# Large products beside a recurrence, issued two k tiles at a time

## The chip, the core and the metric

The kernel runs on one core of a Trainium2 chip. TensorE (PE, its weight loads shown as PEld), VectorE (DVE), ScalarE (ACT), GpSimd (POOL) and the queues of transfers work side by side; each takes its own instructions in order and waits for the others by semaphores. The metric is the device time of one execution in microseconds.

## What is computed

Two layers of a diffusion backbone over 256 context tokens and 512 latent tokens with 1024 channels, in float32. In each layer one input projection feeds three branches: a bidirectional RWKV-7 recurrence of 16 heads of 64, a convolution of width 31, and attention of 8 heads; gates merge them, and an MLP follows. The last layer needs the latent tokens alone. Cut to what matters here:

```python
def _rwkv_scan(state0, r, decay, k, v, kk, a, reverse):
    def step(S, inp):
        r_t, w_t, k_t, v_t, kk_t, a_t = inp
        s_kk = jnp.einsum('bhij,bhj->bhi', S, kk_t)
        S = (S * w_t[:, :, None, :]
             - s_kk[..., None] * (kk_t * a_t)[:, :, None, :]
             + v_t[..., None] * k_t[:, :, None, :])
        return S, jnp.einsum('bhij,bhj->bhi', S, r_t)
    ...
def token_mixer(hc, hl, ..., w_in, ...):
    zc = hc @ w_in          # 1024 x 10112, cut into the branches' parts
    zl = hl @ w_in
```

## The kernel before

All tokens lie along the free axis, channels on partitions. A large product takes 128 columns of a weight: for each of 8 k tiles it multiplies the high and low halves of a split operand and a split weight (`hh,wh`, `hl,wh`, `hh,wl`) in fast float32 (fp32r), so 3 matmuls a k tile and piece of tokens. With all 768 tokens there are two pieces of 384 columns, so 6 matmuls a k tile; with the latent tokens alone one piece of 512, so 3. Weights come in halves of 4 k tiles: ACT rounds one (L328, `wh`), DVE forms the rest (L332, `wl`).

The recurrence is done in chunks of 64 tokens, 12 of them, for a pair of heads at a time; there are 8 pairs a layer, and both directions run together. For each pair: inputs and decays; front groups (L828, six, 64x128 weights) whose masked outputs go to DVE (L832); the inverse of 32x32 blocks on DVE (`rw_solve`, from the transposition L886 over 30 times L891 and L892 to the transpositions L895 and L896); two merges on PE (L928, then L939, 32x32); batches (L955, L966, 64x64); the chain of 12 states (L987, 128x64, and L991, L1006, 64x64, with ACT at L993); and the readout. The next pair's front groups wait for a part of the chain. These small matmuls are plain float32, and most use a part of the array.

While this goes on, the input projection's products are issued as filler. `job` puts a product's 8 k tiles into a list, `fill(n)` issues the next n of them. `weave` runs generators in turns: each tells how many microseconds it has used, `pe` turns them into k tiles by a ratio, and `taps` issues in the same way the convolution's 31 taps of each channel block (L472 and L469, on DVE, pinned behind whatever was written ahead of them). A product's outputs go to its `done` function; for the convolution that is `done_a` (L462 writes `u`, which the taps read), for the recurrence's inputs `shift_done` (shift additions, L656). The attention also calls `fill(1)` between its steps.

The program is not issued in the order in which it is written. A scheduler goes through it and takes for each engine the first instruction that is ready by its own reckoning; among ready ones, what stands earlier in the program comes first, and what is written under high priority comes before the rest.

Of the kernel before, what the change touches and what calls it, by code (L numbers as in the profile page):

```python
# [19 lines left out]
KT = 8  # L20
# [56 lines left out]
class Kern:  # L77
# [319 lines left out]
    def fill(s, n=1):  # L397
        nc = s.nc
        for _ in range(min(n, len(s.jobs))):
            k, mh, ml, T, done, pre = s.jobs.pop(0)  # L400
            if k % 4 == 0:
                while s.halves and len(s.ready) < s.nw:
                    s.ready.append(s.weight_half(*s.halves.pop(0)))
                s.cur = s.ready.pop(0)
            if k == 0:
                s.jps = s.mm()
                s.jctx = (pre(),) if pre else ()
            wh, wl = s.cur
            for w, m, f in ((wh, mh, 0), (wh, ml, 1), (wl, mh, 2)):
                a = m(k)  # L410
                for b, t0, t1 in s.pieces(T):
                    s.last_mm = nc.tensor.matmul(s.jps[:, b, :t1 - t0], lhsT=w[:, k % 4, :], rhs=a[:, t0:t1], start=k == 0 and f == 0, stop=k == KT - 1 and f == 2)  # L412
            if k == KT - 1:
                done(s.jps, *s.jctx)

    def pe(s, us):

        s.debt += us * s.ratio
        n = int(s.debt)
        s.fill(n)  # L420
        s.debt -= n

# [1071 lines left out]
```

## Time and profile before

| | us |
|---|---|
| median of three runs | 4302.82 |
| the runs | 4300.85 to 4306.18 |
| the profiled execution | 4305.05 |
| its span | 4303.3 |
| PE busy | 4083.1 |
| DVE busy | 2712.4 |
| ACT busy | 1829.2 |

The first layer's recurrence lies at about 165 to 1330 us, its attention up to 1535, the merge of the branches and the MLP up to 2486, the second layer's recurrence at 2530 to 3540, its attention up to 3703, and merge and MLP behind it. A row in order of time gives start, duration, engine, line, operation, output and inputs by the program's names, the weights' shape, the shape that streams, and how many such instructions are put together; in brackets the idle time ahead and what ended it. Matmuls overlap, so the time between two starts tells what one costs, not the durations.

### The profile page before, as it was taken

To read this page: it belongs to the slowest core of one execution; us is meant where nothing else is said; L and a number is where in the kernel's file an instruction comes from. 1 tells how busy PE (TensorE), PEld (TensorE's weight loads), DVE (VectorE), ACT (ScalarE), POOL (GpSimd) and SP (SyncE) were. 2 spreads that over 40 slices of the span, in tenths; PEclk is the share of its full clock that TensorE was granted. 3 is DMA by queue.
4 is the path that set the end of the run, shared out by engine and by line. 5 is a ranking of instruction groups with operands and counts; after the bars stand their busy time and mean duration, and the time that the engine had idled before them with its cause. 6 is when DMAs were issued, how large, how long until landed. Compare 5 with 4: busy or idle time off the path is not lost.

```text
span 4303.3 us, 76623 instructions
## 1 busy us (share of the span) xinstructions
PE 4083.1 (95%) x31232; PEld 3360.6 (78%) x31232; DVE 2712.4 (63%) x5126; ACT 1829.2 (43%) x3426; POOL 254.8 (6%) x221
## 2 busy tenths in 40 slices
PE   6999999999998989899999899999999989898998
PEld 4988888888886679689999677877777765575886
DVE  3788888898855554332233478788889855554344
ACT  3444444444434442332222355455555534433332
POOL 0000000000001022100000200000000000121001
PEclk8999999999999999999999899999999979998998
DMA  4212221112134234343332131112122232242332
GB/s 167 80 49 63 59 62 57 49 55 71 58 102 165 70 116 154 126 147 118 101 98 62 64 90 54 55 59 59 59 65 61 84 125 76 68 138 61 96 96 79
DMA packets 443591, 367.70 MB, mean 85 GB/s; under 512 B 19662, under 2 KB 391528, under 8 KB 437096
## 3 DMA queue, kind: packets, MB, share of 16 engines
q1 hardware_dynamic: 422504, 283.10, 21.9%
q10 hardware_dynamic: 20736, 79.70, 5.1%
q8 instruction: 247, 4.05, 0.4%
q14 instruction: 104, 0.85, 0.1%
HBM read 301.38 MB, written 53.48 MB: 82 GB/s over the span
## 4 chain that ended last, share of the span: by engine, by line
PE 78%; DVE 11%; ACT 4%; issue 3%; DMA 2%; POOL 2%; SPq 0%; ACTq 0%; DVEq 0%; POOLq 0%
PE mm L412 29%; PE mm L389 21%; PE g L828 3%; PE g L634 2%; PE g L955 2%; PE g L966 2%; PE sp L987 2%; PE sp L991 2%; PE S L613 1%; PE g L875 1%; PE g L1071 1%; PE yp L1006 1%; DVE wl L332 1%; DVE A L892 1%; DVE Z L891 1%
## 5 line engine op out<-in xcount | busy, mean ns | idle before, releaser
L328 ACT ACTIVATE wh<-raw 128x512 fp32r<-128x512 f32 x700 | 441.4, 631 | 1218.4 <-PE mm L389 562.9
L332 DVE TENSOR_TENSOR wl<-raw,wh 128x512 fp32r<-128x512 f32 x700 | 500.6, 717 | 692.8 <-ACT wh L328 678.6
L412 PE MATMUL mm<-hh,wh 128*128 128x384 f32 (+1 forms) x2072 | 658.9, 378 | 10.0 <-ACT hh L347 4.0
L412 PE MATMUL mm<-hl,wh 128*128 128x384 f32 (+1 forms) x2072 | 626.0, 362 | 7.2 <-POOL hl L330 7.2
L412 PE MATMUL mm<-hh,wl 128*128 128x384 f32 (+1 forms) x2072 | 619.1, 361 | 2.5 <-DVE wl L332 2.4
L472 DVE SCALAR_TENSOR_TENSOR cv<-u,dw,cv 128x783 f32<-128x783 f32 (+1 forms) x480 | 426.7, 889 | 1.5
L412 PEld LDWEIGHTS mm<-hh,wh 128*128 128x128 f32 x2072 | 367.8, 191 | 61.8 <-issue 9.8
L412 PEld LDWEIGHTS mm<-hl,wh 128*128 128x128 f32 x2072 | 383.9, 191 | 34.4 <-POOL hl L330 10.0
L412 PEld LDWEIGHTS mm<-hh,wl 128*128 128x128 f32 x2072 | 384.0, 192 | 29.8 <-DVE wl L332 4.5
L412 PE MATMUL mm<-oh,wh 128*128 128x384 f32 (+1 forms) x768 | 252.3, 383 | 10.4 <-DVE acc L1320 6.0
L412 PE MATMUL mm<-ol,wh 128*128 128x384 f32 (+1 forms) x768 | 240.0, 365 | 10.6 <-POOL ol L330 10.6
L389 PE MATMUL mm<-hh,wh 128*128 128x384 f32 (+1 forms) x768 | 239.1, 366 | 6.3 <-ACT hh L347 3.6
L389 PE MATMUL mm<-hl,wh 128*128 128x384 f32 (+1 forms) x768 | 238.2, 365 | 5.5 <-POOL hl L330 5.0
L412 PE MATMUL mm<-oh,wl 128*128 128x384 f32 (+1 forms) x768 | 239.4, 365 | 0.0
L389 PE MATMUL mm<-hh,wl 128*128 128x384 f32 (+1 forms) x768 | 235.8, 362 | 0.0
L389 PE MATMUL mm<-fh,wh 128*128 128x384 f32 (+1 forms) x768 | 230.0, 353 | 0.0
L389 PE MATMUL mm<-fh,wl 128*128 128x384 f32 (+1 forms) x768 | 229.9, 353 | 0.0
L389 PE MATMUL mm<-fl,wh 128*128 128x384 f32 (+1 forms) x768 | 229.5, 352 | 0.0
L412 PEld LDWEIGHTS mm<-oh,wh 128*128 128x128 f32 x768 | 139.9, 190 | 51.5 <-ACT wh L328 13.6
L993 ACT ACTIVATE S<-sp,lam 128x64 f32<-128x64 f32 x352 | 94.4, 310 | 192.1 <-PE sp L991 172.4
L389 PEld LDWEIGHTS mm<-hh,wh 128*128 128x128 f32 x768 | 142.2, 192 | 37.7 <-ACT wh L328 15.9
L892 DVE TENSOR_TENSOR A<-A,Z 128x30 f32<-128x30 f32 (+14 forms) x480 | 159.0, 331 | 12.2
(300 smaller groups left out, 7078.5 us busy)
## 6 DMA issues: line engine op xcount, KB each, us to landing
raw<-in_w_in_dram SPq DMA_DIRECT2D x316, 256.0 KB
raw<-in_w_ff_dram SPq DMA_DIRECT2D x256, 256.0 KB
wmod<-in_w_mod_dram ACTq DMA_DIRECT2D x48, 1024.0 KB
raw<-in_w_branch_dram SPq DMA_DIRECT2D x96, 256.0 KB
z<-f ACTq DMA_DIRECT2D x40, 384.0 KB
gt<-z SPq DMA_DIRECT2D x24, 384.0 KB
raw<-in_w_out_dram SPq DMA_DIRECT2D x32, 256.0 KB
z<-f ACTq DMA_DIRECT2D x32, 256.0 KB
```

The costliest lines, as they stand in the source:

```text
L328: s.last_hi = nc.scalar.activation(out=hi, in_=src, func=AF.Copy)
L332: nc.vector.tensor_tensor(out=lo, in0=src, in1=hi.bitcast(F32), op=ALU.subtract)
L389: nc.tensor.matmul(ps[:, b, :t1 - t0], lhsT=w[:, k % 4, :], rhs=a[:, t0:t1], start=k == 0 and f == 0, stop=k == KT - 1 and f == 2)
L412: s.last_mm = nc.tensor.matmul(s.jps[:, b, :t1 - t0], lhsT=w[:, k % 4, :], rhs=a[:, t0:t1], start=k == 0 and f == 0, stop=k == KT - 1 and ...
L472: s.tap_pin(nc.vector.scalar_tensor_tensor(out=hold['c'], in0=u[:, k:k + L], scalar=w(k), in1=hold['c'], op0=ALU.mult, op1=ALU.add))
L634: nc.tensor.matmul(op[:, :nq], lhsT=V[:, kk, kv * 128:kv * 128 + 128], rhs=PT[:, kk, :nq], start=kk == 0, stop=kk == nk // 128 - 1)
L828: nc.tensor.matmul(gp[h][:, q, 0:n, :], lhsT=BK[ROWS[h], 4 * g + q].rearrange("p a b -> p (a b)"), rhs=E[ROWS[h], 0:n, 4 * g + q, :], star ...
L892: nc.vector.tensor_tensor(out=X[:, k + 1:, 0:k], in0=X[:, k + 1:, 0:k], in1=tm, op=ALU.add)
L955: nc.tensor.matmul(wu[ROWS[h], q - q0], lhsT=TT[ROWS[h], q, :], rhs=KM[ROWS[h], q].rearrange("p a b -> p (a b)"), start=True, stop=True)
L966: nc.tensor.matmul(ap[ROWS[h], q - q0, 0:n, :], lhsT=W[ROWS[h], q, :], rhs=GB[ROWS[h], h, q, 0:n, :], start=True, stop=True)
L987: nc.tensor.matmul(sp[ROWS[h], d], lhsT=GB[d][:, h, q[d], 0, :], rhs=UV[d][:, h * 12 + q[d], :], start=d == 0, stop=d == 1 and k == 0)
L993: nc.scalar.activation(out=Sn[:, d], in_=sp[:, d], func=AF.Copy, scale=Q['lam', d][:, q[d]:q[d] + 1])
```

## The change

`fill` gathers the matmuls of a k tile in a list. At an even k the first of them is issued as before; the others, and all of the odd k tile that follows, are issued under high priority. `pe` issues only even numbers of k tiles and keeps the odd one as debt. Neither the matmuls nor their operands change.

```diff
--- before.py
+++ after.py
@@ -406,17 +406,23 @@
                 s.jps = s.mm()
                 s.jctx = (pre(),) if pre else ()
             wh, wl = s.cur
-            for w, m, f in ((wh, mh, 0), (wh, ml, 1), (wl, mh, 2)):
-                a = m(k)
-                for b, t0, t1 in s.pieces(T):
-                    s.last_mm = nc.tensor.matmul(s.jps[:, b, :t1 - t0], lhsT=w[:, k % 4, :], rhs=a[:, t0:t1], start=k == 0 and f == 0, stop=k == KT - 1 and f == 2)
+            run = [(w, m, f, p) for w, m, f in ((wh, mh, 0), (wh, ml, 1), (wl, mh, 2)) for p in s.pieces(T)]
+
+            def issue(ps):
+                for w, m, f, (b, t0, t1) in ps:
+                    s.last_mm = nc.tensor.matmul(s.jps[:, b, :t1 - t0], lhsT=w[:, k % 4, :], rhs=m(k)[:, t0:t1], start=k == 0 and f == 0, stop=k == KT - 1 and f == 2)
+            if k % 2 == 0:
+                issue(run[:1])
+                run = run[1:]
+            with s.tc.high_priority():
+                issue(run)
             if k == KT - 1:
                 done(s.jps, *s.jctx)
 
     def pe(s, us):
 
         s.debt += us * s.ratio
-        n = int(s.debt)
+        n = int(s.debt) // 2 * 2
         s.fill(n)
         s.debt -= n
```

In the changed program L412 becomes L413, and each later line's number is higher by 6.

Two places in the order. PE in the first layer's recurrence, in the chain of states (`sp`, `yp`) beside batches (`GB`, `BK`); `mm` are the large products. Before:

```order
L412 MATMUL mm<-hh,wh 128x384
L966 MATMUL g<-GB_683,BK_680 64x128 x8
L412 MATMUL mm<-hh,wh 128x384
L412 MATMUL mm<-hl,wh 128x384 x2
L412 MATMUL mm<-hh,wl 128x384 x2
L1040 MATMUL g<-cst,y 128x128 x3
L987 MATMUL sp<-UV_679,GB_678 64x64 x2
L987 MATMUL sp<-UV_684,GB_683 64x64 x2
L991 MATMUL sp<-S,KR_676 64x64 x2
L991 MATMUL sp<-S,KR_681 64x64 x2
L1006 MATMUL yp<-S,KR_676 64x64 x2
L1006 MATMUL yp<-S,KR_681 64x64 x2
```

In the changed program, in the same part:

```order
L413 MATMUL mm<-hh,wl 128x384 x2
L713 MATMUL g<-cst,A 128x128 x3
L972 MATMUL g<-GB_678,BK_675 64x128 x8
L993 MATMUL sp<-UV_679,GB_678 64x64 x2
L993 MATMUL sp<-UV_684,GB_683 64x64 x2
L997 MATMUL sp<-S,KR_676 64x64
L972 MATMUL g<-GB_683,BK_680 64x128 x8
L997 MATMUL sp<-S,KR_676 64x64
L997 MATMUL sp<-S,KR_681 64x64 x2
L1012 MATMUL yp<-S,KR_676 64x64 x2
L1012 MATMUL yp<-S,KR_681 64x64 x2
L413 MATMUL mm<-hh,wh 128x384 x2
```

Runs of one to six large matmuls between small groups have become runs of twelve; the small groups between them stand together, and a batch now stands inside a step of the chain. Over the whole program PE goes from a small group to large products 953 times before and 547 times now.

DVE in the inverse of the sixth pair of the first layer; `A` and `Z` are its two buffers, `cv` is the convolution's sum. Before:

```order
L891 TENSOR_TENSOR Z<-A 128x108
L892 TENSOR_TENSOR A<-A,Z 128x27x4
L332 TENSOR_TENSOR wl<-raw,wh 128x512
L891 TENSOR_TENSOR Z<-A 128x130
L892 TENSOR_TENSOR A<-A,Z 128x26x5
L891 TENSOR_TENSOR Z<-A 128x150
L892 TENSOR_TENSOR A<-A,Z 128x25x6
```

In the changed program:

```order
L898 TENSOR_TENSOR A<-A,Z 128x19x12
L475 TENSOR_SCALAR cv<-u,dw,V 128x783
L897 TENSOR_TENSOR Z<-A 128x234
L478 SCALAR_TENSOR_TENSOR cv<-u,dw,cv 128x783
L898 TENSOR_TENSOR A<-A,Z 128x18x13
L478 SCALAR_TENSOR_TENSOR cv<-u,dw,cv 128x783
L897 TENSOR_TENSOR Z<-A 128x238
L478 SCALAR_TENSOR_TENSOR cv<-u,dw,cv 128x783
```

Before, splits of weights stand between the steps of this inverse and no tap; now taps alternate with the steps, 21 of them in this pair, and shift additions stand there too.

## Rows read from the trace of the kernel before

**Rows 1.** The page's part 1: engine, busy us (share of the span) xinstructions.

```profile
PE 4083.1 (95%) x31232; PEld 3360.6 (78%) x31232; DVE 2712.4 (63%) x5126; ACT 1829.2 (43%) x3426; POOL 254.8 (6%) x221
```

**Rows 2.** Windows of both recurrences: length, then busy us of PE, PEld, DVE, ACT, POOL.

```profile
223.00:1195.00 972.00, 966.86 (x10051) 834.72 (x10050) 838.48 (x1595) 471.69 (x945) 11.68 (x28) 0.99 0.19 59
2592.00:3441.00 849.00, 824.35 (x8647) 654.56 (x8649) 715.59 (x1502) 451.06 (x918) 8.08 (x28) 0.98 0.21 62
```

**Rows 3.** PE in order of time, first layer: start, us, what it is, xcount.

```profile
895.07 1.15 PE L875 MATMUL g<-UV,GL 64*64 64x64 f32 x32
896.15 0.62 PE L412 MATMUL mm<-hh,wh 128*128 128x384 f32 x2
896.61 0.51 PE L412 MATMUL mm<-hl,wh 128*128 128x384 f32 x2
896.95 0.51 PE L412 MATMUL mm<-hh,wl 128*128 128x384 f32 x2
...
898.43 0.68 PE L875 MATMUL g<-UV,GL 64*64 64x64 f32 x16
899.05 0.62 PE L412 MATMUL mm<-hh,wh 128*128 128x384 f32 x2
...
940.79 0.44 PE L412 MATMUL mm<-hh,wh 128*128 128x384 f32 x1
941.16 1.09 PE L955 MATMUL g<-BK,GL 64*64 64x128 f32 x16
```

**Rows 4.** The same view, small groups behind one another.

```profile
957.42 0.45 PE L987 MATMUL sp<-UV,GB 128*64 128x64 f32 x8
957.70 0.86 PE L1001 MATMUL yp<-UV,GB 128*64 128x64 f32 x22
...
962.79 0.45 PE L987 MATMUL sp<-UV,GB 128*64 128x64 f32 x8
963.17 0.45 PE L991 MATMUL sp<-S,KR 64*64 64x64 f32 x8
```

**Rows 5.** The same view, sixth pair: end of its front groups, and its merge.

```profile
877.55 0.62 PE L412 MATMUL mm<-hh,wh 128*128 128x384 f32 x2
...
913.15 0.95 PE L928 MATMUL g<-Z,GL 32*32 32x32 f32 x48
```

**Rows 6.** DVE in order of time, the inverse of the sixth pair.

```profile
881.01 2.07 DVE L886 STREAM_TRANSPOSE A<-Z 128x1024 f32<-128x1024 f32 x1 [0.75 <-ACT Z L863]
...
891.91 0.39 DVE L892 TENSOR_TENSOR A<-A,Z 128x220 f32<-128x220 f32 x1
892.33 0.40 DVE L891 TENSOR_TENSOR Z<-A 128x228 f32<-128x228 f32 x1
892.64 0.68 DVE L332 TENSOR_TENSOR lw<-lraw,lw 128x512 fp32r<-128x512 f32 x1
893.24 0.39 DVE L892 TENSOR_TENSOR A<-A,Z 128x228 f32<-128x228 f32 x1
...
911.89 2.03 DVE L896 STREAM_TRANSPOSE Z<-A 128x1024 f32<-128x1024 f32 x1
```

**Rows 7.** PE in order of time, second layer, sixth pair: front's end, merge.

```profile
3160.07 0.50 PE L412 MATMUL mm<-hl,wh 128*128 128x512 f32 x1
...
3199.07 0.95 PE L928 MATMUL g<-Z,GL 32*32 32x32 f32 x48 [0.73 <-DVE Z L895]
```

**Rows 8.** What L928 waited for (us, times), whole span, then the second recurrence.

```profile
  DVE Z L895: 15.4, 16
...
  DVE Z L895: 13.7, 14
```

**Rows 9.** Lines L472 (first, second layer) and L656: ns min/median/max, first and last start.

```profile
L472 DVE SCALAR_TENSOR_TENSOR cv<-u,dw,cv x240: 994/1030/1049, 227.3 to 1233.9; 128x783 f32<-128x783 f32 x120
...
L472 DVE SCALAR_TENSOR_TENSOR cv<-u,dw,cv x240: 711/748/773, 2570.6 to 3470.9; 128x512 f32<-128x512 f32 x120
...
L656 DVE SCALAR_TENSOR_TENSOR E<-f,H,E x56: 465/608/753, 225.1 to 1074.1; 128x255 f32<-128x255 f32 x28, 128x511 f32<-128x511 f32 x28
```

**Rows 10.** The same view, weight loads of the large products.

```profile
L412 PEld LDWEIGHTS mm<-hh,wh x2072: 186/188/338, 69.3 to 3522.1; 128*128 128x128 f32 x189
```

## Prediction

> **What bounds the kernel now.** I read the busy times first, then the two recurrence stretches as windows, then one pair of heads on PE and on DVE in order of time, then what the first merge of a pair waits for. PE is busy for 95% of the span [rows 1]. In the recurrence of the first layer it is busy 966.9 of 972 us and DVE 838.5; in the second layer 824.4 and 715.6 of 849 [rows 2]. So PE is the wall and DVE stands at 86% and 84%, near behind it.
>
> A pair of heads goes round one loop on these two. PE issues the six front groups (L828); when the last is through, DVE runs the inverse, a chain of 60 steps between L886 and L896; then PE may issue the merge (L928), later the chain of states, and then the next pair's front groups. While DVE inverts, PE has little but large products (L412). The reader should see that the two are nearly equal now. In the sixth pair of the first layer PE goes from the end of its front groups at 877.55 to the merge at 913.15, 35.6 us, without a wait [rows 5], and DVE needs from 881.01 to about 913.9 [rows 6]. In the sixth pair of the second layer PE is 0.73 us early and waits for Z L895 [rows 7]; 14 of the 16 such waits, 15.4 us in all, are in that layer [rows 8].
>
> **What the change saves: borders on PE.** No matmul is added or taken out. A small product works on a part of the array (64x64, 64x128, 128x64, 32x32), a large one on all of it, and a change between shapes has a price. Two L412 in a dense run start 0.345 us after the two before them (896.61 to 896.95), the first two behind a small group 0.46: 0.11 lost. The small group itself gives up its place late: 32 matmuls of L875 take 1.08 us, 16 take 0.62, so the last 16 take 0.16 more than the 16 ahead of them [rows 3]. An entry into a run of large products costs 0.27 by these rows; I take 0.25, since groups of other shapes lose a little less. One single L412 between two small groups takes 0.37 [rows 3]: 0.1735 of its own, 0.11 of the entry, 0.09 for the exit. From one small shape to another: eight L987 take 0.38 us ahead of L991, which has another shape, and 0.28 ahead of L1001, which has the same [rows 4], so 0.10; mixed with full-array products it is nearer to the 0.16 of an entry, and I take 0.15.
>
> Now the counts, over both orders whole. Entries with a change of shape go from 654 to 398, exits from 593 to 346; small to small with a change of shape rises from 564 to 774, because small groups that were kept apart now stand side by side. 256 x 0.25 = 64 us and 247 x 0.09 = 22 us are saved, 210 x 0.15 = 31 us are added: **55 us saved**, 35 of it in the first layer. Ends: with 0.10 for small to small 65, with 0.27 (a whole entry) 29. The change of shape to full-array small products (L724, L842) costs nothing in the rows and is left out.
>
> **What the change costs: the inverse on DVE.** Nothing in the diff touches DVE, but the order of its instructions moves. Large products run ahead of the recurrence, at most pairs' front groups by 24 to 151 more of them than before, so the inputs of the convolution come at other times; its taps (L472, 31 a pair), which stood between the merge and the next front groups, where DVE waits for PE anyway, now stand between the steps of the inverse. PE's own work in that stretch becomes less, since a run of twelve now stands behind each front group (72 products there in the first layer, 23 to 39 before) and is missing later. Both together make PE wait at the merge.
>
> How long DVE needs, from the end of the front groups to the merge: two steps of the inverse start 0.42 us apart (891.91, 892.33); with a 0.68 us split between them 0.91 (892.33 to 893.24) [rows 6]. So what is put between steps costs its duration less 0.19: 0.5 for a split, 0.84 for a tap of 1.03 in the first layer, 0.56 for one of 0.748 in the second, about 0.4 for a shift addition (L656) of 0.61 [rows 9]. The bare rest I take from the sixth pair of the second layer, where DVE was last: 3160.07 to 3199.07 is 39.0 us [rows 7]; its 7 splits, 5 taps, 6 shift additions and one short step are 9.0; 30.0 stays. How much PE has there: the sixth pair of the first layer has 150 large products, 150 x 0.1735 = 26.0 of its 35.6 us, so 9.6 for the small ones [rows 3, 5]; in the second layer 146 products and 9.6 make 38.3, so 0.197 a product (two widths) [rows 7].
>
> Taps inside the inverse, pair by pair, before: 0 in pairs 1 to 7 and 8 in pair 8 of the first layer; 15, 5, 0, 10, 11, 5, 11, 8 in the second. Now: 2, 19, 2, 6, 6, 21, 6, 0 and 16, 14, 18, 18, 13, 7, 14, 1. Large products between front and merge, before: 149 to 179, and 115 to 166. Now: 144, 184, 144, 192, 180, 120, 192, 132 and 168, 192, 114, 108, 120, 108, 132, 108. Two pairs in full. First layer, pair 6: 21 taps, 12 shift additions and 3 splits are 17.6 + 4.8 + 1.5 = 23.9, DVE needs 53.9; PE has 9.6 + 120 x 0.1735 = 30.4; PE waits 23.5. Second layer, pair 4: 18 taps, 10 additions, 6 splits are 17.1, DVE needs 47.1; PE has 9.6 + 108 x 0.197 = 30.9; it waits 16.2. The same for all: 1.8, 10.6, 1.8, 0.4, 2.5, 23.5, 0.4, 1.1 = 42 us in the first layer; 4.2, 0, 15.5, 16.2, 11.6, 10.0, 9.2, 5.2 = 72 us in the second. Less the 15 us of such waits that are there now, **99 us are added**. They can't be won back elsewhere: where the taps are gone, PE's queue sets the pace, and it keeps its order. The ends are a tap at 0.7 times its price and small work of 12 us (some 45 us) and full durations without the 0.19 (some 135).
>
> **Sum:** -55 + 99 = +44 us on the profiled execution's 4305.05, which is 2.2 above the median of the runs: **4347 us**. First layer +5, second +39. The attention (1 k tile at a time at L623, now in twos) and the MLP have no change of shape and get nothing.
>
> **Rivals.** *Faster:* only the borders count. If DVE's taps inside the inverse find PE busy after all, because products behind the merge's place cover it, 4303 - 55 = 4248. For it: PE is the wall nearly everywhere. Against it: PE takes its queue in order, and the merge stands ahead of those products. It decides if the new waits stay under 46 us. *Even:* new waits of 46 to 63 us beside that saving, 4294 to 4311. *Slower still:* the cover at the end is gone too. After the last merge of the first layer 360 large products stood ahead of the attention, now 252, so 108 x 0.1735 = 19 us of the last pair's chain may stand bare, 6 us in the second layer, and every front group waits behind up to 2.1 us of a run: 25 to 60 us more, 4370 to 4405. Against it: PE's work there is only moved, not lost. *The border has no price:* large products gain nothing from standing together, and only the waits stay, 4303 + 99 = 4402. Rows speak against it: two L412 start 0.17 apart [rows 3] while each load of weights takes 0.188 [rows 10], so loads do overlap in a run and not at its ends. The Trainium skill (TensorE: Matmul & The Clock Gate, "Part 3: Packing small matmuls") says that a weight load overlaps running matmuls only where the row group differs; by it a run would be no cheaper than its pieces, which is this rival. The trace disagrees by those 0.17 us.
>
> **How the numbers follow.** Forecast 0.60 (its own range 4315 to 4370), faster 0.12, even 0.09, slower still 0.15, no price 0.04. A measurement tells about 0.2% from no change, so 4294 to 4311 counts as the same: faster 0.12, same 0.09, slower 0.79. The range 4296 to 4405 leaves out the faster case and the top of the last two.
>
> **What would show it.** Right: the merge's waits for Z L895 grow from 14 us to some 110, the longest over 15 us in the sixth pair of the first layer; taps stand between the inverse's steps; PE's busy time in the recurrences falls by 50 us or so while the stretches get longer; DVE's busy time stays. Borders wrong: the first two products behind a small group no longer 0.46 apart. Waits wrong: merges that wait a us or less in pairs 3 to 6 of the second layer; then the time falls to about 4250.

## The result and the profile after

| | before | after |
|---|---|---|
| median of four runs, us | 4304.5 | 4379.14 |
| the runs, us | 4300.85 to 4308.1 | 4373.76 to 4386.62 |
| the profiled execution, us | 4305.05 | 4386.62 |
| its span, us | 4303.3 | 4384.8 |

The ratio is 1.0175 (95% interval 1.0156 to 1.0193): 75 us slower. The forecast had the sign, but was 32 us short.

The page's part 1 of after, against [rows 1]: PE is busy for 34 us less and DVE for 8 less, while the span is 81.5 us longer.

```profile
PE 4049.4 (92%) x31232; PEld 3381.0 (77%) x31232; DVE 2704.9 (62%) x5126; ACT 1833.5 (42%) x3426; POOL 256.9 (6%) x221
```

Windows of after, cut here and in all that follows from the first merge of a layer to the first merge of its eighth pair (window, length, then busy us of PE, PEld, DVE, ACT, POOL, granted clock, DMA share, GB/s), and the same of before with those exact ends, close to [rows 2]:

```profile
228.73:1220.83 992.10, 947.18 (x10110) 848.24 (x10111) 827.82 (x1595) 474.71 (x945) 11.22 (x28) 0.96 0.19 59
2612.39:3521.10 908.71, 831.94 (x8650) 667.97 (x8649) 718.20 (x1500) 450.94 (x918) 7.94 (x28) 0.96 0.20 59
```

```profile
223.09:1195.12 972.03, 966.77 (x10052) 834.72 (x10051) 838.60 (x1595) 471.60 (x945) 11.68 (x28) 0.99 0.19 59
2592.21:3440.79 848.58, 824.14 (x8634) 654.35 (x8635) 715.17 (x1501) 451.06 (x918) 8.08 (x28) 0.98 0.21 62
```

The first stretch is 20.1 us longer and the second 60.1, 80.2 of the 81.5 us. PE's idle time there (length less busy) goes from 5.3 to 44.9 and from 24.4 to 76.8 us, 92 more. And the granted clock falls from 0.99 and 0.98 to 0.96.

What PE waited for in the second of these stretches, after (engine, line, releaser: us, times, longest); its third line answers to [rows 8], where it was 13.7 us:

```profile
PE mm L413 <- DVE wl L332: 33.2, 15, 6.4
PE mm L413 <- ACT cv L460: 6.8, 4, 2.8
PE g L934 <- DVE Z L901: 5.3, 5, 1.6
PE g L834 <- DVE E L821: 4.8, 4, 1.4
```

So the merge (now L934) waits no longer than before. PE sits inside a run of large products, for a rest of a weight (`wl`) that DVE has not made yet; over the whole span such waits come to 60.6 us. The sixth pair of the first layer, PE in order of time (start, us, what it is; in brackets the idle time ahead and its releaser); it stands against [rows 5]:

```profile
900.33 1.16 PE L834 MATMUL g<-E,BK 64*128 64x128 f32 x16
...
931.86 0.62 PE L413 MATMUL mm<-hh,wh 128*128 128x384 f32 x2 [1.87 <-ACT in_v L659]
932.32 0.51 PE L413 MATMUL mm<-hl,wh 128*128 128x384 f32 x2
942.15 1.01 PE L413 MATMUL mm<-hh,wl 128*128 128x384 f32 x2 [9.32 <-DVE wl L332]
942.96 0.84 PE L413 MATMUL mm<-hh,wh 128*128 128x384 f32 x2
943.60 0.84 PE L413 MATMUL mm<-hl,wh 128*128 128x384 f32 x2
944.24 0.84 PE L413 MATMUL mm<-hh,wl 128*128 128x384 f32 x2
...
947.82 0.51 PE L413 MATMUL mm<-hh,wl 128*128 128x384 f32 x2
950.62 0.81 PE L413 MATMUL mm<-hh,wl 128*128 128x384 f32 x2 [2.29 <-DVE wl L332]
...
954.73 0.51 PE L413 MATMUL mm<-hh,wh 128*128 128x384 f32 x2
955.08 0.51 PE L413 MATMUL mm<-hl,wh 128*128 128x384 f32 x2
955.42 0.51 PE L413 MATMUL mm<-hh,wl 128*128 128x384 f32 x2
955.87 0.31 PE L934 MATMUL g<-Z,GL 32*32 32x32 f32 x8
```

DVE in the same pair, against [rows 6]:

```profile
904.21 1.95 DVE L892 STREAM_TRANSPOSE A<-Z 128x1024 f32<-128x1024 f32 x1 [1.27 <-ACT Z L869]
...
939.94 0.35 DVE L898 TENSOR_TENSOR A<-A,Z 128x198 f32<-128x198 f32 x1
940.22 1.02 DVE L478 SCALAR_TENSOR_TENSOR cv<-u,dw,cv 128x783 f32<-128x783 f32 x1
941.16 0.33 DVE L897 TENSOR_TENSOR Z<-A 128x184 f32<-128x184 f32 x1
941.42 0.67 DVE L332 TENSOR_TENSOR wl<-raw,wh 128x512 fp32r<-128x512 f32 x1
942.02 0.33 DVE L898 TENSOR_TENSOR A<-A,Z 128x184 f32<-128x184 f32 x1
...
952.47 2.04 DVE L901 STREAM_TRANSPOSE Z<-A 128x1024 f32<-128x1024 f32 x1
```

The same end in the sixth pair of the second layer, DVE's transposition and PE's merge:

```profile
3268.14 1.94 DVE L901 STREAM_TRANSPOSE Z<-A 128x1024 f32<-128x1024 f32 x1
3270.13 0.95 PE L934 MATMUL g<-Z,GL 32*32 32x32 f32 x48 [1.64 <-DVE Z L901]
```

The reader should see four things. From the end of the front groups (901.2) to the merge it is 54.7 us, with taps between the steps, as the prediction had it (53.9). The idle time stands in the middle, not at the merge: the split at 941.42 has its turn behind the steps and taps ahead of it, and ends the wait of 9.32 us. And after that wait two large products start 0.64 us apart, where they start 0.345 apart in [rows 3] and again from 954.73 on: PE runs at 1.2 GHz in place of 2.4 until 947.5, and once more after the wait at 950.62. Nothing in the prediction's sum stands for that. Last, the merge starts as soon as DVE is through: 0.05 us after the end of the transposition in the second layer's pair, 1.36 us after it in the first layer's. In ten of the fourteen merges that end a loop in these stretches it is 0.05 to 0.17 us, in the other four 0.5 to 1.4.

### The profile page after: what moved, and what is told of

It reads as the page before. It is cut to its first block, busy times and chain, and to the rows that moved or that the text cites. A ratio compares the mean times of both kernels' runs of the same rounds, so it can differ in the third digit from the quotient of the medians.

```text
span 4384.8 us, 76693 instructions
## 1 busy us (share of the span) xinstructions
PE 4049.4 (92%) x31232; PEld 3381.0 (77%) x31232; DVE 2704.9 (62%) x5126; ACT 1833.5 (42%) x3426; POOL 256.9 (6%) x221
## 5 line engine op out<-in xcount | busy, mean ns | idle before, releaser
L413 PE MATMUL mm<-hh,wh 128*128 128x384 f32 (+1 forms) x2072 | 655.1, 380 | 19.7 <-ACT cv L460 6.8
L413 PE MATMUL mm<-hh,wl 128*128 128x384 f32 (+1 forms) x2072 | 615.4, 361 | 59.3 <-DVE wl L332 59.1
L413 PE MATMUL mm<-hl,wh 128*128 128x384 f32 (+1 forms) x2072 | 612.7, 360 | 6.5 <-POOL hl L330 6.5
L413 PEld LDWEIGHTS mm<-hh,wl 128*128 128x128 f32 x2072 | 391.9, 195 | 90.5 <-DVE wl L332 68.8
L413 PEld LDWEIGHTS mm<-hh,wh 128*128 128x128 f32 x2072 | 374.9, 195 | 66.2 <-ACT cv L460 7.3
L413 PEld LDWEIGHTS mm<-hl,wh 128*128 128x128 f32 x2072 | 393.1, 195 | 24.3 <-POOL hl L330 9.0
L413 PE MATMUL mm<-oh,wh 128*128 128x384 f32 (+1 forms) x768 | 250.5, 381 | 8.0 <-ACT oh L328 5.0
L413 PE MATMUL mm<-ol,wh 128*128 128x384 f32 (+1 forms) x768 | 236.7, 363 | 11.3 <-POOL ol L330 11.3
L389 PE MATMUL mm<-hl,wh 128*128 128x384 f32 (+1 forms) x768 | 237.7, 364 | 5.4 <-POOL hl L330 4.9
L413 PE MATMUL mm<-oh,wl 128*128 128x384 f32 (+1 forms) x768 | 235.4, 361 | 1.5 <-DVE wl L332 1.5
L413 PEld LDWEIGHTS mm<-oh,wh 128*128 128x128 f32 x768 | 140.8, 191 | 44.0 <-ACT wh L328 14.6
L389 PEld LDWEIGHTS mm<-hh,wh 128*128 128x128 f32 x768 | 141.7, 191 | 37.6 <-ACT wh L328 15.9
L413 PEld LDWEIGHTS mm<-ol,wh 128*128 128x128 f32 x768 | 142.1, 191 | 33.7 <-POOL ol L330 21.3
```

Source lines behind the costliest of these rows:

```text
L389: nc.tensor.matmul(ps[:, b, :t1 - t0], lhsT=w[:, k % 4, :], rhs=a[:, t0:t1], start=k == 0 and f == 0, stop=k == KT - 1 and f == 2)
```

## The experiments

Two readings serve all of them, both over the two stretches named above. **PE's work** is the length less PE's idle time less what the clock took while PE was busy, (1 - granted clock) x time over PE's busy time. (A clock that is low while PE stands idle takes nothing from it; in the changed kernel that is 10.4 of the 71.7 us that the granted clock of the two stretches tells.) **The prediction's two models** are applied to each kernel's order with no price changed: borders (0.25 an entry, 0.09 an exit, 0.15 small to small), counted here inside the two stretches, where they give the change 47.1 of its 55 us, and waits (inverse against PE's work in the same place). The table with all kernels stands at the end.

**Runs without the taps.** Taps 1 to 30 are left out (a part of the convolution isn't computed) in the changed kernel and in the one before:

```diff
-            s.cops = [tap0] + [lambda k=k: tap(k) for k in range(1, CONV_W)] + [store]
+            s.cops = [tap0] + [store]
```

> The changed kernel with the convolution's taps 1 to 30 left out of each channel block (only the first tap is computed, so the convolution's output is not the reference's). It is read against the unchanged order without the same taps (e6_before_notaps). The order gives 400 entries into and 351 exits from large products with a change of shape, 707 changes between small shapes, and no more than one tap in any inverse. Theory (borders cost what the prediction says; the loss is PE idle behind a DVE that is stretched by taps, and the lower clock after that idle): waits of 15 us in place of 118, clock in the recurrences back at 0.98 or more, and a time 50 to 65 us below e6_before_notaps, some 4235 us. Rival (borders have little price, or the runs of twelve hurt by themselves): within 15 us of e6_before_notaps, or above it.

> The kernel before with the same taps 1 to 30 left out (the convolution's output is not the reference's). 688 entries, 642 exits, 406 changes between small shapes. Both theories: PE is the wall with or without taps, so the time falls little, by 0 to 25 us, to some 4280 to 4305 us. If it falls by far more, taps cost the kernel before more than its waits show.

Measured: 4249.17 and 4249.38 us, equal. The expectation missed twice. Before without taps fell by 50 us, so the taps cost that kernel more than its waits show. And the changed order kept nothing, which is what the rival said. The windows (e5, then e6) say why:

```profile
224.41:1166.79 942.38, 919.87 (x10015) 831.62 (x10016) 638.53 (x1375) 470.35 (x940) 11.72 (x28) 0.97 0.20 60
2562.20:3385.27 823.07, 803.59 (x8612) 656.90 (x8613) 590.08 (x1293) 447.08 (x913) 9.39 (x28) 0.97 0.21 63
```

```profile
222.07:1172.99 950.92, 946.99 (x10012) 819.37 (x10012) 638.30 (x1377) 471.92 (x942) 9.44 (x28) 0.99 0.20 59
2568.16:3386.68 818.52, 803.40 (x8628) 640.79 (x8629) 593.47 (x1295) 448.38 (x912) 8.58 (x28) 0.99 0.21 63
```

PE's work is 60.9 us less in e5 (borders by the prediction: 45.7). But PE idles 22.9 us more and loses 34.0 more to the clock, 32.3 of it between a merge and the next front groups, where PE is busy for 98% of the time. The idle time is in small pieces. PE in e5, first layer, in order of time:

```profile
482.91 0.51 PE L413 MATMUL mm<-hh,wl 128*128 128x384 f32 x2
484.51 0.95 PE L934 MATMUL g<-Z,GL 32*32 32x32 f32 x48 [1.09 <-DVE Z L901]
486.47 1.49 PE L934 MATMUL g<-Z,GL 32*32 32x32 f32 x48 [1.01 <-DVE Z L902]
487.89 1.01 PE L413 MATMUL mm<-hh,wh 128*128 128x384 f32 x2
488.69 0.84 PE L413 MATMUL mm<-hl,wh 128*128 128x384 f32 x2
489.33 0.84 PE L413 MATMUL mm<-hh,wl 128*128 128x384 f32 x2
...
499.63 0.59 PE L413 MATMUL mm<-hl,wh 128*128 128x384 f32 x2
500.06 0.51 PE L413 MATMUL mm<-hh,wl 128*128 128x384 f32 x2
```

Two waits of a microsecond, and the large products behind them run at half the clock up to 499.6. So the two readings of "equal" stand against each other: no border price, or a border price given back. The next run tells them apart.

**Shorter runs.** One k tile in place of two, with the taps and without:

```diff
-            if k % 2 == 0:
-                issue(run[:1])
-                run = run[1:]
+            issue(run[:1])
+            run = run[1:]
...
-        n = int(s.debt) // 2 * 2
+        n = int(s.debt)
```

> The change with runs of one k tile in place of two: the first matmul of every k tile is issued as before, its other five (two in the second layer) at high priority, and the debt is not made even. The order gives 533 entries, 460 exits and 638 changes between small shapes, which at the prediction's prices is 31 us less than before; the taps in the inverses stand nearly as before (0 in pairs 1 to 7), and the model of the waits gives 32 us against 23. Theory: 22 us faster than before, 4275 to 4290, clock as before (0.97). Rival (runs have no price, only waits count): 4305 to 4320.

> e9_one with the convolution's taps 1 to 30 left out (the convolution's output is not the reference's). 559 entries, 498 exits, 480 small to small, which is 34 us less than e6_before_notaps by the prices; the model of the waits gives 29 us against 26. Theory (e5_after_notaps, equal in time to e6_before_notaps, did the same recurrence work in 62 us less, and gave that back as 22 us more idle and 36 us more lost to the clock behind gaps of 1 to 2 us; shorter runs leave both as in e6_before_notaps): 20 to 32 us faster than e6_before_notaps, 4217 to 4230. Rival (changes of shape have no price, and that is why those two are equal): 4245 to 4255 again.

Measured: e13 4225.87 us, 23.5 below e6, inside the theory's 4217 to 4230; the rival (4245 to 4255) falls. With the taps, e9 takes 4287.24, 0.9971 of before (0.9958 to 0.9983), 12.5 us faster and within the theory's bounds. In the two stretches its work is 29.4 us less (prices 25.9), and it gives 14.7 back as idle and 13.8 to the clock, the clock's part all in the second layer. That leaves 0.9 us there; most of what the profiled execution gained lies outside the stretches, nearly 8 us of it in the first layer's attention, for which the prediction had nothing. e13 does 37.6 us less work than e6 in the stretches (prices 29.8) and is 6.0 us shorter there; the larger part of its gain lies outside, too. So PE's work does fall with the changes of shape, about as the prediction prices them. The prediction tied its rival without a border price to a line of the Trainium skill (TensorE: Matmul & The Clock Gate, "Part 3: Packing small matmuls"): a weight load overlaps running matmuls only where the row group differs. e13 isn't equal to e6, as that rival would have it; the section's own text also lets a load into the background weight buffer go ahead.

**The late splits.** Is it the rest of the weight that comes too late, or DVE as a whole? In the changed kernel:

```diff
-        s.split(wh, wl, raw, s.lo_pool)
+        with s.tc.high_priority():
+            s.split(wh, wl, raw, s.lo_pool)
```

> The changed kernel with the splits of the weights (ACT's rounding and DVE's rest) issued at high priority too, so that they go ahead of taps that wait in front of DVE. In the changed kernel PE waits 60.6 us for such rests in front of its large products, and hardly at the merge. Theory (DVE as a whole needs longer from front to merge than PE has work; the rests are only where PE meets that): the model's waits are 116 us, as in the changed kernel (118), so the time stays within 15 us of 4379 and the waits go to the merge's wait for Z. Rival (it is the late rests themselves that cost): the 60 us go, time 4310 to 4330.

Measured: 4422.04 us, 1.029 (1.0271 to 1.0309). The rival falls clearly, and the theory's "within 15 us" falls too: 43 us slower than the changed kernel. What PE waited for in the second stretch (line numbers are higher by one more here), and what ACT's copy `f` waited for itself, over the whole span:

```profile
PE mm L414 <- ACT f L1119: 32.3, 6, 9.0
PE mm L414 <- ACT cv L461: 13.4, 5, 3.9
...
ACT f L1119 <- DVE in_v L663: 44.0, 9, 9.1
```

The waits for `wl` are gone, and PE's idle time is what it was, 122.0 against 121.7 us. About 20 us went to the merge, as I expected (its waits for Z are 48.7 us over the whole span, 28.3 in the changed kernel). The larger part went to ACT, whose copies out of PSUM (`f`) stand waiting in turn for shift additions (`in_v`) that have their place between DVE's steps. So the place of a wait tells little here; behind the largest of them is DVE again. The stretches are 28.7 us longer, 19.9 of them between front groups and merge, where the merge again starts within 0.7 us of the end of DVE's transposition and DVE waits 10.6 us longer inside the inverses, for ACT. The clock takes 22.2 us more of PE's busy time, 16.8 of them in that same part.

**The two halves of the change**, the even debt alone and the high priority alone:

```diff
-        n = int(s.debt)
+        n = int(s.debt) // 2 * 2
```

> The half of the change that makes the debt even, alone: two k tiles are issued together, nothing at high priority. The order moves little: 601 entries (654 before), 564 exits (593), 575 small to small (564), which is 14 us less by the prediction's prices; the model of the waits gives 27 us against 23. Theory (borders are priced and what hurts comes from the high priority): 0 to 15 us faster, 4285 to 4300. Rival (it is the pairing that hurts): over 4320.

```diff
...
+            if k % 2 == 0:
+                issue(run[:1])
+                run = run[1:]
+            with s.tc.high_priority():
+                issue(run)
```

> The other half alone: the high priority over two k tiles, with the debt as before. 383 entries, 316 exits, 801 small to small: 57 us less by the prices. The model of the waits gives 92 us (before 23, the whole change 118). Theory (idle as the model has it, and beside it the time that the lower granted clock after a wait costs, about half as much as the added idle by the whole change: 44 us lost to the clock on 90 us of idle): -57 + 69 + 35, so 4335 to 4360. Rival (the sum of the prediction without the clock): 4305 to 4320.

Measured: the even debt alone 4289.04, 0.9975 (0.9963 to 0.9986), 12 us faster, as expected. The high priority alone 4373.44, 1.017 (1.0156 to 1.0183), 13 us above the theory's range and 53 above its rival's. Idle 73.5 us more than before (model 69), work 39 less (prices 49), and 39.1 more to the clock, where I had reckoned 35. So the loss is the high priority's. Making the debt even gains 12 us alone and nothing that shows beside the high priority (ratio 1.0175 with it, 1.017 without).

**The taps moved, nothing left out.** The convolution's two products go ahead of the pair's spills in the queue, in the changed kernel and, as a control, in the one before; and in e9:

```diff
-                    spills(todo_c(p + 1) - todo_c(p))
                     s.conv_jobs(l, P, p + 1, T, s.ocv)
+                    spills(todo_c(p + 1) - todo_c(p))
```

> The changed kernel with the two products of the convolution queued ahead of the pair's spills instead of behind them, nothing left out; so the taps' input is there earlier and fewer taps stand in the inverses (the longest runs fall from 21 and 18 to 19 and 16, most to 3 to 14, beside more large products there). The order gives 381 entries, 338 exits, 759 small to small: 62 us less than before. The model of the waits gives 60 us (before 23, changed kernel 118). Theory (what the changed kernel lost is idle behind inverses stretched by taps, and the clock behind that idle; in runs of one kernel a granted clock lower by 0.004 goes with 13 us more, about 0.7 us for each us lost): -62 + 37 + some 13 for the clock, 4280 to 4300, so some 90 us faster than the changed kernel. Rival (runs of twelve hurt by themselves): 4350 or more.

> The kernel before with the same exchange of queues, as a control: 632 entries, 564 exits, 567 small to small (8 us less), waits by the model 47 us against 23. Theory: -8 + 24 + some 9 for the clock, 4315 to 4335, slower than before. Rival (the exchange is a gain by itself, whatever the runs): below 4300.

> e9_one (runs of one k tile) with the same exchange of queues: 490 entries, 429 exits, 636 small to small, 45 us less than before; the model of the waits gives 44 us. Theory: -45 + 21 + some 8 for the clock, 4278 to 4292. Rival (the sum by borders and waits doesn't rank orders that lie this near): above 4300 or below 4270.

Measured: e14 4341.92 (1.0096, 1.0079 to 1.0113), e16 4331.94 (1.0082, 1.0064 to 1.0099), e15 4299.41 (1.0, 0.9988 to 1.0012). The same exchange that costs the kernel before 34 us makes the changed one 37 us faster, since it takes taps out of its inverses and puts some into the other's (7 or 8 in each of pairs 3 to 7 of the first layer, where there were none). That is the mechanism's sign in both. The sizes: e16 as expected; e14 42 us above its range and 8 below its rival's bound, e15 7 above its range and a microsecond below its rival's. In e14 idle is 54 us above before, where the model gives 37, and the clock takes 39.6 more; in e15 it takes 37.7 more. Behind the merge, where the model has nothing, e14 idles 20.5 us more than before and loses 29.9 more to the clock. The waits were many and short (some 35 over 0.25 us in e14's first stretch, 5 in that of before), which the model doesn't see.

**A version that beats both.** Runs of one k tile where e9's stretch became shorter (products over all tokens, so the first layer), and then also the even debt there:

```diff
+            n = 1 if T == TOK else len(run)
+            issue(run[:n])
+            run = run[n:]
```

> Runs of one k tile at high priority, as in e9_one, for products over all 768 tokens alone (the first layer's recurrence above all); those over the latent tokens alone, the second layer's, are issued as before. e9_one's trace has the first layer's recurrence 12 us shorter than before at an unchanged clock (0.993), the second layer's 11 us longer with a clock of 0.958 against 0.978. Theory (a run gains only where it opens no waits): both good halves together, 20 to 25 us faster than before, 4275 to 4282. Rival (the layers aren't separate; what the first gains the second loses whatever its order): 4287 or more.

```diff
+        s.pair = 2 if T == TOK else 1
...
+        n = int(s.debt) // s.pair * s.pair
```

> e12_one_layer1 with the debt made even in the first layer's recurrence: 546 entries, 469 exits, 643 small to small, 26 us less than before (e12_one_layer1 21); the model of the waits gives 35 us, as there (33). Theory: 3 to 5 us below e12_one_layer1, 4275 to 4283. Rival: no better than it, 4283 or more.

Measured: e12 4282.82 (0.9954, 0.9943 to 0.9966), 18 us faster than before and a microsecond off its range; e17 4274.11 (0.9941, 0.9927 to 0.9955), 24 us faster and a microsecond below its range, the best here. Both keep the clock of before (27.2 and 28.6 us lost; before 26.9). Of e17's gain 18.9 us lie in the two stretches.

**All kernels**, us in the two stretches of the profiled execution; "clock" is what it took while PE was busy, "model" and "borders" are the prediction's two models on each order (with the mean duration of every line in place of the rounded ones, the waits of after come to 118 where the prediction has 42 + 72):

| kernel | length | idle | model | clock | work | borders | work less borders |
|---|---|---|---|---|---|---|---|
| before | 1820.6 | 29.7 | 23 | 26.9 | 1764.0 | 246.3 | 1517.7 |
| after | 1900.8 | 121.7 | 118 | 61.3 | 1717.8 | 199.2 | 1518.6 |
| e1 even | 1817.6 | 33.7 | 27 | 30.4 | 1753.5 | 232.8 | 1520.8 |
| e2 high | 1894.6 | 103.2 | 92 | 66.0 | 1725.5 | 197.7 | 1527.8 |
| e3 splits | 1929.5 | 122.0 | 116 | 83.5 | 1724.0 | 191.7 | 1532.3 |
| e9 one | 1819.7 | 44.4 | 32 | 40.7 | 1734.6 | 220.4 | 1514.3 |
| e12 one, layer 1 | 1808.6 | 39.0 | 33 | 27.2 | 1742.5 | 228.4 | 1514.0 |
| e14 conv first | 1861.9 | 83.9 | 60 | 66.5 | 1711.6 | 193.8 | 1517.8 |
| e15 one, conv first | 1840.4 | 55.8 | 44 | 64.6 | 1720.1 | 207.9 | 1512.2 |
| e16 before, conv first | 1854.8 | 45.0 | 47 | 48.7 | 1761.1 | 240.3 | 1520.8 |
| e17 one, even, layer 1 | 1801.7 | 42.7 | 35 | 28.6 | 1730.4 | 222.7 | 1507.7 |
| e5 after, no taps | 1765.5 | 42.0 | 15 | 52.8 | 1670.7 | 190.1 | 1480.6 |
| e6 before, no taps | 1769.4 | 19.1 | 26 | 18.8 | 1731.6 | 235.8 | 1495.9 |
| e13 one, no taps | 1763.4 | 40.9 | 29 | 28.5 | 1694.0 | 206.0 | 1488.0 |

In the eleven kernels that compute everything the work ranges over 52 us, and the work less the border price over 25. The prices are wrong by most in e3, which does 40 us less work than before where they give 55. Leaving out the taps takes 32 us of PE's work from the kernel before and 47 from the changed one, of which the prices explain 11 and 9, though the taps aren't on PE; what the rest is stays open.

## Why the prediction was right, and why it was short

**The wall and the loop** held: a DVE that is busy for 718 of 909 us made PE wait, and of the span's 81.5 us 80.2 lie in the two loops. What settles it is the length of each loop from the end of the front groups to the merge, against the rest of the loop (both stretches, seven loops in each, us):

| | before | after | added |
|---|---|---|---|
| front groups to merge | 534.0 | 601.0 | 67.0 |
| of it PE idle | 9.1 | 85.2 | 76.1 |
| of it taken by the clock while PE was busy | 0.0 | 29.6 | 29.6 |
| merge to the next front groups | 1286.6 | 1299.8 | 13.2 |
| of it PE idle | 20.6 | 36.5 | 15.9 |
| of it taken by the clock while PE was busy | 26.9 | 31.7 | 4.8 |

**Borders, -55 us:** of these, 47.1 lie in the two stretches by the same prices, and PE's work fell by 46.2 there. Outside of them nothing was gained: all that lies ahead of, between and behind the stretches is 1.3 us longer. By layer the prices are less sure: 40 in the first, where they give 32, and 6 in the second, where they give 15. The sign for a wrong price wasn't seen: two products behind a small group still take 0.45 us in the first layer (median at the full clock, before and after).

**The stretched inverse, +99 us:** held. In the fourteen loops the prediction has 108 us of waits between front groups and merge; PE idled there for 85.2 and lost 29.6 to the clock, 114.8 in all. The two belong together, since DVE sets the length of this part: the merge follows DVE's transposition by 4.9 us in all fourteen loops together, and DVE stands idle inside these inverses for 9.2 us in all, mostly for ACT. While PE has to wait for DVE anyway, a lower clock takes the place of waiting. The place of the waits did not hold: what was to be seen, the merge's waits for Z L895 growing to some 110 us, is wrong. All merges of after wait 28.3 us for DVE's two transpositions (before 22.4), and the time is lost earlier, where large products of the run need a rest that waits on DVE behind taps. PE's queue holds the merge behind those products, so the loop is the same.

**The step that failed is the sum,** which puts all of the new waits ahead of the merge and nothing behind it, saying that there PE's queue sets the pace. Behind the merge PE idled 15.9 us more, mostly in waits of 0.7 to 3 us for DVE, ACT and a transfer, and lost 4.8 more to the clock. These 20.7 us, the 9 us of borders that did not come, 7 more us ahead of the merge and the 1.3 outside are the 37 us between the forecast's 44 and the 81.5 measured. (In the second layer a loop's rest behind the merge is longer by 31.7 us in sum; most of that is work which no longer stands ahead of the merge, and the sum has counted it as waits there.)

**The clock** is no term of that sum either, and it fell: it took 34.4 us more of PE's busy time in the two stretches, -46.2 + 92.0 + 34.4 = 80.2. But 29.6 of them lie ahead of the merge, where they cost at most some 14 us, the 4.9 by which the merges came late and the 9.2 for which DVE waited. It does cost where PE is the wall: in e5, 32.3 us behind the merges are the larger part of what ate the gain. Of 45 runs of the kernel before, the 3 at a granted clock of 0.967 have a mean span of 4307.5 us, the 10 at 0.971 of 4293.9; 13.6 us for some 17 lost, and over all 45 some 0.7 us go with each. I had [rows 2] with 0.99 and 0.98 and did not ask what 92 us of waits would do to them.

**Luck:** 4379 lies above the forecast's own range (4315 to 4370). It lies inside the whole range only by the room made for *slower still*, which is not what happened.

**DVE's busy time stays:** right (2712.4, 2704.9). **PE's busy time in the recurrences falls by 50 us or so:** it fell by 11.8, since products at half the clock are busy for longer (-46.2 + 34.4).

**The rivals.** *Faster* and *even* fell with the waits. *No border price* gives 4402, too high, and e13 speaks against it. *Slower still* has the time (4370 to 4405), but not its main cause: the end of a layer isn't bare. Behind the last first merge of the second layer 863.7 us are left against 862.5, and between the layers' loops 1391.6 against 1397.1, so nothing was lost there. Its other half, front groups that stand behind a run, no run tells apart from the 20.7 us found behind the merges.

What stays open: why the waits behind the merges come, in after and most of all in e14, and what decides which of the short waits the clock answers; in after's second stretch a wait of 2.8 us passed without it, and in e5 two of a microsecond did not.

## What to carry to other kernels

Where an engine is the wall and another stands at 85% of it in the same loop, changing the order of the first moves the second's work as well: look through the order of both, and count what is put inside the other's chain of dependent steps. A wait that an edit opens on TensorE can cost twice, as idle time and as a lower clock behind it, but the second price depends on the place. Ahead of the merge, where DVE set the pace, the lower clock took the place of waiting; where TensorE was the wall, in e5, waits of a microsecond or two and the clock behind them gave back 57 of the 61 us saved. It has no fixed rate: e12 idled 9.3 us more than before and lost 0.3 more to the clock, e15 26.1 more and lost 37.7. So apply such an edit only where the trace shows that it opens few waits: a milder form of this one, in one layer alone, gave 24 us.

## What the runs showed of the hardware

A wait of a microsecond or two on TensorE can be followed by more than ten at 1.2 GHz (e5: 1.09 and 1.01 us of waiting, then large products 0.64 us a pair until 499.6 in place of 0.345). Over the whole span the granted clock tells of 134.9 us lost before (3.1%) and 196.3 after (4.5%), of which 106.5 and 149.7 fell while PE was busy; in runs of one program the granted clock differs from 0.967 to 0.973. The Trainium skill (TensorE: Matmul & The Clock Gate, "Part 1: The HAM clock gate") puts the penalty of the ramp, which it describes at a kernel's start, under 1% of a typical span for modelling. A clock that falls again and again in the middle, as here, isn't in that figure and has to be read from the trace.
